# Three stick-breaking steps per pair of heads, and the first sparse unit at a higher priority

## Chip, cores and metric

The kernel runs on one core of a Trainium2 chip. The metric is the device time of one execution in microseconds. Five engines work side by side: TensorE (PE, matmuls; its weight loads are shown as PEld), VectorE (DVE), ScalarE (ACT), GpSimd (POOL) and SyncE (SP, which issues most transfers). Sums of matmuls lie in PSUM, which the kernel divides into eight banks of 128 x 512 values: two called `acc`, four called `S`, one `o` and one `tp`.

## What is computed

Two layers, each with two token mixers on the same normalised input of 512 tokens by 1024. The reference, cut to what matters:

```python
def stick_breaking_attention(q, k, v):           # 8 heads of 64
    for i in range(s_len // Q_BLOCK):
        ...
        z = einsum('bhqd,bhkd->bhqk', qb, kb) * scale
        mask = s[None, :] < t[:, None]
        log_1m = where(mask, log_sigmoid(-z), 0.0)
        between = cumsum(log_1m, axis=3, reverse=True) - log_1m
        w = where(mask, exp(log_sigmoid(z) + between), 0.0)
        outs.append(einsum('bhqk,bhkd->bhqd', w, vb))

def nsa_attention(...):                          # 8 query heads, 2 key heads
    kc, vc = compress_blocks(...)                # 31 blocks, two-layer MLP
    p_cmp = masked_softmax(q @ kc)               # o_cmp = p_cmp @ vc
    ...                                          # selected blocks: all 8 are taken
    o = gates[0] * o_cmp + gates[1] * o_slc + gates[2] * o_win

def hybrid_layer(x, ...):
    proj = rms_norm(x, norm_g) @ w_in            # 5912 columns
    y_a = merge_heads(o_a) * silu(sb_z)
    y_b = o_b * silu(n_z)
    merged = sigmoid(gate_a) * (y_a @ w_up_a) + sigmoid(gate_b) * (y_b @ w_up_b)
    return x + merged @ w_out
```

## The kernel before

Tokens stand along the columns and channels along the partitions. The projections are made from weights split into a high part `whi` (a cast on GpSimd or ScalarE, L162 and L404) and a low part `wlo` (VectorE, L404), three matmuls per block of 128 channels, into the banks `acc`. `w_ahead` keeps three splits ahead of TensorE.

A layer has three stages. In the first, the stick-breaking of four pairs of heads runs beside projections; in the second, the sparse attention of four query heads per key head runs beside the gate projections; in the third come the up projection and the output projection.

TensorE's order is written out by the kernel: `Pacer` counts estimated microseconds (`tick`), holds generators of projections (`fill`) and a list of steps that fall due after a given latency (`due`). `pump(us)` takes fill until that much planned time has gone by; `until` takes fill until a condition holds. The other engines' instructions are put in order by priority: `high_priority(offset=...)` moves them ahead of what has a smaller offset, PRIO is 300, PRIO_SB 600, PRIO_EV 900.

**Stick-breaking.** A pair of heads has four steps, from key block 3 (128 query columns) to block 0 (512). Step t makes the logits (`sb_qk`: two heads, a correction and a main matmul each, in one bank S per head), after which VectorE takes the mask's minimum (L903), ScalarE makes |z|, exp and log(1 + .) (L904 to L906), and VectorE adds (L907) into `e`. `sb_split` splits `e` into high and low parts and adds up, on GpSimd, the columns of the blocks seen (`sum`). `sb_cs` subtracts sums on TensorE with a triangular matrix for the own block and a matrix of ones for the blocks above, and ScalarE makes the weights `w`. `sb_pv` multiplies with the values into bank o. The loop at the end of the listing runs one round per step: values of step t-2, logits of step t, `X_GAP[0]` of fill, sums of step t-1, split of step t, `X_GAP[1]` of fill; 18 rounds with 3.5 + 3.4 planned us.

**Value tiles and compression.** `prep_vs` makes the stick's values `vS` (tile `gv`) in two halves, each of four token tiles (`proj_tok`), which VectorE evacuates at L659. `prep_cmp` lays out the compression's input (`f_t`, L691, 16 additions a layer), `prep_mlp`, `mlp_act`, `mlp_t`, `mlp_w2` and `mlp_k` are its chain down to the compressed keys `kC` (L799 to L803), with latencies `LAT` between them. `norm_rope` normalises a projection; its `rest` step uses the bank tp, and so do `mlp_t`, `mlp_w2`, `mlp_k` and `cmp_qk`.

**Passage to the sparse stage.** After the loop come `cmp_qk(0)`, the compression scores, and `nsa_qk(0, UNITS[0])`, the logits of the first unit (query blocks 0 and 1), which fill four banks S: two key heads by two query blocks. For each key head VectorE masks (L1047) and takes maxima (L1048), ScalarE makes exponentials `pr` (L1055), VectorE scales (L1065). `Y_LAT` planned us later the next unit's logits take the banks.

## Time and profile before

| | us |
|---|---|
| median of three runs (1001.96 to 1002.39) | 1002.15 |
| the profiled execution | 1003.2 |
| its span, first to last instruction | 1001.5 |
| TensorE busy | 967.7 |
| VectorE busy | 701.9 |
| ScalarE busy | 467.3 |
| GpSimd busy | 208.9 |

In the profile a line names source line, engine, operation, and the tiles as out<-in. "Idle before" is the time in which the engine stood still before an instruction, with what ended it. Ends of matmuls are modelled, so two matmuls in a row seem to overlap. The granted clock of TensorE is given as a share of 2.4 GHz.

### The profile page before, as it was taken

What the parts mean: (1) busy time and instruction counts of PE and PEld (TensorE: products, weight loads), DVE (VectorE), ACT (ScalarE), POOL (GpSimd) and SP (SyncE); (2) the same over time, 40 slices, a digit from 0 to 9 for tenths busy, and PEclk for the clock granted to TensorE, in tenths of its full rate; (3) what the DMA queues carried; (4) which work ended last, traced back from release to release, by engine and by line L of the source; (5) the groups of instructions that cost most, each with busy time, mean ns of one, the idle gap of its engine ahead of it and who ended that gap; (6) DMA issues with size and microseconds to landing.
All of it is one profiled execution on the core that took longest, in us unless ns stands there. A gap on an engine that the chain in (4) does not pass through costs nothing.

```text
span 1001.5 us, 14850 instructions
## 1 busy us (share of the span) xinstructions
PE 967.7 (97%) x5315; PEld 769.1 (77%) x5315; DVE 701.9 (70%) x1398; ACT 467.3 (47%) x1139; POOL 208.9 (21%) x256
## 2 busy tenths in 40 slices
PE   6999999989999999999999999999899999999998
PEld 4776767767888888888888787686688888888886
DVE  6778758779968875566565985587996887655631
ACT  5656355554543444533343535565453544344321
POOL 4153235431101111000012532343111101100000
PEclk9999999898999999999999999999899999999999
DMA  9433246422212222353643224363222221224331
GB/s 284 118 90 100 59 126 156 101 64 53 64 47 60 64 64 63 85 144 98 189 122 95 85 80 124 102 144 93 52 61 64 64 54 53 64 85 143 89 116 53
DMA packets 167530, 94.36 MB, mean 94 GB/s; under 512 B 39568, under 2 KB 160672, under 8 KB 167456
## 3 DMA queue, kind: packets, MB, share of 16 engines
q1 hardware_dynamic: 163120, 88.14, 32.7%
q10 hardware_dynamic: 3632, 3.17, 1.3%
q0 software_dynamic: 704, 2.11, 0.5%
q8 instruction: 42, 0.69, 0.3%
q14 instruction: 32, 0.26, 0.1%
HBM read 80.81 MB, written 6.29 MB: 87 GB/s over the span
## 4 chain that ended last, share of the span: by engine, by line
PE 76%; DVE 13%; ACT 6%; issue 3%; DMA 1%; POOL 1%; SPq 0%; ACTq 0%; DVEq 0%; POOLq 0%
PE acc L345 48%; PE S L345 16%; PE o L345 6%; PE tp L349 4%; DVE f_t L691 2%; DVE wlo L404 2%; PE tp L345 2%; ACT e L215 1%; ACT e L905 1%; DVE sX L505 1%; DVE hl L590 1%; DVE spl L923 1%; DVE sp L923 1%; DMA x_sb<-in_x_dram 1%; DVE e L907 1%
## 5 line engine op out<-in xcount | busy, mean ns | idle before, releaser
L345 PE MATMUL acc<-hh,whi 128*128 128x512 f32 x640 | 257.2, 402 | 0.1
L345 PE MATMUL acc<-hl,whi 128*128 128x512 f32 x640 | 255.0, 399 | 1.7 <-DVE hl L590 1.4
L345 PE MATMUL acc<-hh,wlo 128*128 128x512 f32 x640 | 181.7, 408 | 0.0
L162 POOL TENSOR_SCALAR whi<-raw 128x1024 fp32r<-128x1024 f32 (+1 forms) x84 | 95.0, 1130 | 400.1 <-PE acc L345 322.3
L404 DVE TENSOR_TENSOR wlo<-raw,whi 128x1024 fp32r<-128x1024 f32 (+1 forms) x124 | 154.9, 1249 | 32.7 <-POOL whi L162 23.0
L345 PEld LDWEIGHTS acc<-hl,whi 128*128 128x128 f32 x640 | 120.6, 188 | 27.4 <-DVE hl L590 3.4
L345 PEld LDWEIGHTS acc<-hh,whi 128*128 128x128 f32 x640 | 120.8, 189 | 26.3 <-issue 2.5
L345 PEld LDWEIGHTS acc<-hh,wlo 128*128 128x128 f32 x640 | 119.4, 191 | 27.6 <-issue 3.6
L404 ACT CAST whi<-raw 128x1024 fp32r<-128x1024 f32 x40 | 42.0, 1050 | 128.0 <-PE acc L345 47.5
L1078 ACT ACTIVATE pT<-tp 128x512 f32<-128x512 f32 x80 | 48.1, 601 | 102.5 <-PE tp L349 101.5
L1055 ACT ACTIVATE pr<-S,mx 128x256 f32<-128x256 f32 x192 | 81.9, 446 | 17.4 <-DVE mx L1048 10.3
L1048 DVE TENSOR_REDUCE mx<-S 128x2 f32<-128x512 f32 (+1 forms) x96 | 55.3, 593 | 11.8 <-PE S L345 11.7
L215 ACT ACTIVATE e<-S 128x128 f32<-128x128 f32 (+3 forms) x64 | 25.3, 435 | 80.4 <-DVE S L903 76.3
L345 PE MATMUL acc<-whi,hh 128*128 128x256 f32 (+1 forms) x192 | 58.0, 302 | 3.6 <-DVE gv L659 3.3
L1065 DVE TENSOR_SCALAR pr<-pr,rc 128x128 f32<-128x128 f32 (+3 forms) x128 | 55.0, 471 | 1.1
L345 PE MATMUL acc<-wlo,hh 128*128 128x256 f32 (+1 forms) x192 | 55.7, 290 | 0.0
L345 PE MATMUL acc<-whi,hl 128*128 128x256 f32 (+1 forms) x192 | 55.6, 290 | 0.0
L345 PE MATMUL S<-yh,wlo 128*128 128x512 f32 x128 | 50.7, 396 | 0.0
L345 PE MATMUL S<-yh,whi 128*128 128x512 f32 x128 | 50.7, 396 | 0.0
L345 PE MATMUL S<-yl,whi 128*128 128x512 f32 x128 | 50.1, 392 | 0.0
L349 PE MATMUL tp<-identf,pr 128*128 128x128 f32 x320 | 49.3, 277 | 0.0
L345 PE MATMUL S<-kN,nX 64*128 64x512 f32 (+1 forms) x192 | 42.2, 407 | 6.8 <-ACT pr L1055 6.8
(316 smaller groups left out, 1778.2 us busy)
## 6 DMA issues: line engine op xcount, KB each, us to landing
raw<-in_w_in_dram SPq DMA_DIRECT2D x72, 512.0 KB, 3.9
raw<-in_w_in_dram SPq DMA_DIRECT2D x36, 256.0 KB, 3.7
raw<-in_cmp_w_dram SPq DMA_DIRECT2D x16, 512.0 KB, 4.1
raw<-in_w_out_dram SPq DMA_DIRECT2D x16, 512.0 KB, 4.1
raw<-in_w_up_a_dram SPq DMA_DIRECT2D x16, 256.0 KB, 3.2
raw<-in_w_up_b_dram SPq DMA_DIRECT2D x32, 128.0 KB, 3.3
gv<-xs SPq DMA_DIRECT2D x16, 256.0 KB, 2.8
sq<-xq SPq DMA_DIRECT2D x48, 64.0 KB, 2.0
```

Source lines behind the costliest of these rows:

```text
L162: G.tensor_scalar(dst, src, 1.0, 0.0, op0=ALU.mult, op1=ALU.add)
L215: ins = A.activation(dst, src, func, **kw)
L345: T.matmul(out, lhsT, rhs, start=start, stop=stop, **kw)
L349: T.transpose(out, in_, ident)
L404: for ins in (eng.copy(hi, rv), V.tensor_sub(lo, rv, hi.bitcast(F32))):
L505: V.tensor_sub(X[b, g], q[a], X[a, g].bitcast(F32))
L691: V.tensor_tensor(f_v[hf][t * HD:(t + 1) * HD, :, a, g, 0:NCMP], src[:, :, t, hf:hf + NCMP], pe_v[:, hf * 8:(hf + 1) * 8, t:t + 1].to_broa ...
L923: V.tensor_sub(sp[1], e[:, :n], sp[0].bitcast(F32))
L1048: V.tensor_reduce(mx[:, n, g], sb[g][n].rearrange("p (k t c) -> p t k c", t=2, c=P), axis=AX.XY, op=ALU.max, negate=True)
L1055: exps.append(A.activation(pr[g][:, o:o + b - a, t], sv[:, t], AF.Exp, bias=mx[:, 0 if one else n, g, t:t + 1], accum_out=dn[:, n, g, t:t ...
L1065: V.tensor_scalar(pr[g][:, o:e, t], pr[g][:, o:e, t], rc[:, n, g, t:t + 1], None, op0=ALU.mult)
L1078: A.activation(pT.rearrange("p g t q -> p (g t q)"), pt, AF.Copy)
```

## The change

- The stick's steps per pair become three (`STEPS`): blocks 3 and 2 side by side in one bank (128 and 256 columns), then block 1, then block 0. `sb_qk`, `sb_split`, `sb_cs`, `sb_sum` and `sb_pv` follow. The loop has 14 rounds with 4.6 + 4.1 planned us.
- `cmp_qk(0)` and the first unit's `nsa_qk` stand under offset 600, and the next unit falls due one planned us later.
- The first two value tiles of the first half use banks S.
- The first half of the feature blocks is put off as well, by 0.0 and 1.5 us, and the second by 5.0 and 7.0.
- `ht` and `hv2` share a tile of the pool `wk`. The zeroing of `kC` moves ahead of its evacuation, which stands under offset 900. Three latencies grow.

```diff
@@ -38,12 +38,13 @@
 PRIO = 300
...
 N_WARM = (3, 2, 2, 3)
-LAT = {'norm': 5.0, 'mlp_t': 9.0, 'mlp_w2': 3.5, 'mlp_k': 16.0, 'sb0': 3.8, 'sb': 4.5, 'ang': 1.5, 'sin': 0.5}
+LAT = {'norm': 5.0, 'mlp_t': 11.5, 'mlp_w2': 4.2, 'mlp_k': 16.0, 'sb0': 3.8, 'sb': 5.7, 'ang': 1.5, 'sin': 0.5}
 PRIO_SB = 600
 PRIO_EV = 900
-X_GAP = (3.5, 3.4)
+X_GAP = (4.6, 4.1)
+STEPS = ((3, 2), (1,), (0,))
 Y_GAP = 1.5
-F_GAP = ((6.0, 8.0), (5.0, 7.0))
+F_GAP = ((0.0, 1.5), (5.0, 7.0))
 Y_LAT = (9.8, 9.2, 10.2)
@@ -445,12 +446,12 @@
         yield from gemm(po, wh, wl, hs.hh, hs.hl)
...
 
-    def proj_tok(l, pieces, evac):
+    def proj_tok(l, pieces, evac, bank_of=lambda i: acc_bank()):
         n = sum(m for _, m in pieces)
...
         for i in range(NT):
-            po = acc_bank()
+            po = bank_of(i)
             sl = slice(i * P, (i + 1) * P)
@@ -659,7 +660,7 @@
                         V.tensor_scalar(vS[i][:, c * 256:(c + 1) * 256], po[:, :256], r_col[:, i:i + 1], None,
...
 
-                yield from proj_tok(l, VS_P[c], evac_s)
+                yield from proj_tok(l, VS_P[c], evac_s, lambda i: s_bank() if c == 0 and i < 2 else acc_bank())
                 done.add(("vs", c))
@@ -694,8 +695,8 @@
                                     pe_v[:, hf * 8:(hf + 1) * 8, t:t + 1].to_broadcast([HD, 8, NCMP]),
...
 
-                        block(0)
-                        pc.later(F_GAP[a][g], lambda block=block: block(1))
+                        pc.later(F_GAP[0][g], lambda block=block: block(0))
+                        pc.later(F_GAP[1][g], lambda block=block: block(1))
 
@@ -749,9 +750,10 @@
                     pt = t_bank()
...
                         tr(pt[:, t * P:(t + 1) * P], u1[:, t * P:(t + 1) * P], identf)
-                    ht = g_tile("w", n=256).rearrange("p (t c) -> p t c", t=2)
+                    h4 = wkt("h4")
+                    ht = h4[:, :256].rearrange("p (t c) -> p t c", t=2)
                     V.tensor_copy(ht.rearrange("p t c -> p (t c)"), pt[:, :256])
-                    hv2 = g_tile("w", n=256).rearrange("p (t a c) -> p t a c", t=2, a=2)
+                    hv2 = h4[:, 256:].rearrange("p (t a c) -> p t a c", t=2, a=2)
                     for t in range(2):
@@ -796,11 +798,13 @@
                     pt = t_bank()
...
                     ptv = pt[:, 0:HD].rearrange("p (g c) -> p g c", g=2)
+                    for g in range(2):
+                        V.memset(kC[(1 - g) * HD:(2 - g) * HD, g, 1].bitcast(F32), 0.0)
+                with tc.high_priority(offset=PRIO_EV):
                     A.activation(kC[:, :, 0], ptv, AF.Copy)
                     for g in range(2):
-                        a, b = slice(g * HD, (g + 1) * HD), slice((1 - g) * HD, (2 - g) * HD)
+                        a = slice(g * HD, (g + 1) * HD)
                         V.tensor_sub(kC[a, g, 1], ptv[a, g], kC[a, g, 0].bitcast(F32))
-                        V.memset(kC[b, g, 1].bitcast(F32), 0.0)
                     done.add("cmp")
@@ -885,89 +889,107 @@
                     V.tensor_mul(g, po, r_bc)
...
 
+            def sb_step(t):
+                j, s = t // len(STEPS), t % len(STEPS)
+                cols_of, n = [], 0
+                for kb in STEPS[s]:
+                    cols_of.append((kb, slice(n, n + S - kb * P)))
+                    n += S - kb * P
+                return j, s, cols_of, n
+
             def sb_qk(t):
-                j, kb = t // NT, NT - 1 - t % NT
+                j, s, cols_of, n = sb_step(t)
                 R = sb_in[j]
-                n = S - kb * P
-                ks = slice(kb * P, (kb + 1) * P)
                 zb = [s_bank() for _ in range(2)]
-                for h, z in enumerate(zb):
-                    gs = slice(h * HD, (h + 1) * HD)
-                    mm(z[:, :n], R.sK2[gs, ks], R.sX[gs, h, kb * P:], True, False, n * .00022)
-                for h, z in enumerate(zb):
-                    mm(z[:, :n], R.sK1[:, h, ks], R.sX[:, h, kb * P:], False, True, n * .00043)
+                for kb, c in cols_of:
+                    ks = slice(kb * P, (kb + 1) * P)
+                    for h, z in enumerate(zb):
+                        gs = slice(h * HD, (h + 1) * HD)
+                        mm(z[:, c], R.sK2[gs, ks], R.sX[gs, h, kb * P:], c.start == 0, False, (S - kb * P) * .00022,
+                           skip_group_check=True)
+                for kb, c in cols_of:
+                    ks = slice(kb * P, (kb + 1) * P)
+                    for h, z in enumerate(zb):
+                        mm(z[:, c], R.sK1[:, h, ks], R.sX[:, h, kb * P:], False, True, (S - kb * P) * .00043,
+                           skip_group_check=True)
                 with tc.high_priority(offset=PRIO_SB):
...
                         e = g_tile("e")
-                        V.tensor_tensor(z[:, :P], z[:, :P], mk_sb, op=ALU.min)
+                        m = len(cols_of)
+                        zd = z[:, :m * P].rearrange("p (m c) -> p m c", m=m)
+                        V.tensor_tensor(zd, zd, mk_sb[:, None, :].to_broadcast([P, m, P]), op=ALU.min)
                         act_exp(e[:, :n], z[:, :n], AF.Abs)
...
                         R.e[h] = e
-                R.z[kb] = zb
+                R.z[s] = zb
 
             def sb_split(t):
-                j, kb = t // NT, NT - 1 - t % NT
+                j, s, cols_of, n = sb_step(t)
                 R = sb_in[j]
-                n = S - kb * P
                 with tc.high_priority(offset=PRIO_SB):
...
                         e = R.e[h]
-                        sp = [g_tile(f"sp{t}0", F32R) if kb == 0 else px.tile([P, n], F32R, tag=f"sp{t}{kb}", name="sp", bufs=2)
+                        sp = [g_tile(f"sp{t}0", F32R) if s == 2 else px.tile([P, n], F32R, tag=f"sp{t}{s + 1}", name="sp", bufs=2)
                               for t in "hl"]
-                        ins = A.activation(sp[0], e[:, :n], AF.Copy)
+                        ins = A.activation(sp[0][:, :n], e[:, :n], AF.Copy)
                         for i in w_last:
                             order(ins, i)
-                        V.tensor_sub(sp[1], e[:, :n], sp[0].bitcast(F32))
-                        R.sp[h, kb] = sp
-                        if kb == NT - 1:
+                        V.tensor_sub(sp[1][:, :n], e[:, :n], sp[0][:, :n].bitcast(F32))
+                        R.sp[h, s] = sp
+                        if s == 0:
                             R.sum[h] = px.tile([P, 2 * P], F32, tag="sum", name="sum", bufs=2)
-                            copy_pool(R.sum[h][:, P:], e[:, :P])
-                        elif kb > 0:
-                            G.tensor_add(R.sum[h][:, P * (kb - 1):], R.sum[h][:, P * (kb - 1):], e[:, P:n])
-                            if kb == 2:
-                                copy_pool(R.sum[h][:, :P], e[:, :P])
+                            G.tensor_add(R.sum[h][:, P:], e[:, :P], e[:, 2 * P:n])
+                            copy_pool(R.sum[h][:, :P], e[:, P:2 * P])
+                        elif s == 1:
+                            G.tensor_add(R.sum[h], R.sum[h], e[:, P:n])
 
             def sb_cs(t):
-                j, kb = t // NT, NT - 1 - t % NT
+                j, s, cols_of, n = sb_step(t)
                 R = sb_in[j]
-                n = S - kb * P
-                R.w[kb] = []
+                R.w[s] = []
                 for h in range(2):
-                    z = R.z[kb][h]
-                    for kk in (kb + 1, kb) if kb < NT - 1 else (kb,):
-                        off = (kk - kb) * P
+                    z = R.z[s][h]
+                    sp = R.sp[h, s]
+                    if s == 0:
+                        parts = [(ntri, sp, slice(0, P), slice(0, P)), (nones, sp, slice(0, P), slice(2 * P, 3 * P)),
+                                 (ntri, sp, slice(P, 3 * P), slice(P, 3 * P))]
+                    else:
+                        parts = [(nones, R.sp[h, s - 1], slice(P * (2 - s), 3 * P), slice(P, n)),
+                                 (ntri, sp, slice(0, n), slice(0, n))]
+                    for m, (tri, src, a, b) in enumerate(parts):
                         for u in range(2):
-                            mm(z[:, off:n], ntri if kk == kb else nones, R.sp[h, kk][u], False,
-                               kk == kb and u == 1, 0.04 + (n - off) * .00034, skip_group_check=True)
+                            mm(z[:, b], tri, src[u][:, a], False, m == len(parts) - 1 and u == 1,
+                               0.04 + (b.stop - b.start) * .00034, skip_group_check=True)
                     w = g_tile("w")
...
                         w_last.append(act_exp(w[:, :n], z[:, :n], AF.Exp))
-                    R.w[kb].append(w)
-                if 0 < kb < NT - 1:
+                    R.w[s].append(w)
+                if s < 2:
                     for h in range(2):
-                        sb_sum(R, h, kb, n - P)
-
-            def sb_sum(R, h, kb, n):
-                h0, l0 = (u[:, P:] for u in R.sp[h, kb])
-                s = R.sum[h][:, P * (kb - 1):] if kb == 2 else R.sum[h]
+                        sb_sum(R, h, s)
+
+            def sb_sum(R, h, s):
+                c = slice(2 * P, 3 * P) if s == 0 else slice(P, 3 * P)
+                h0, l0 = (u[:, c] for u in R.sp[h, s])
+                sm = R.sum[h][:, P:] if s == 0 else R.sum[h]
                 with tc.high_priority(offset=PRIO_SB):
-                    copy_pool(h0, s)
-                    G.tensor_sub(l0, s, h0.bitcast(F32))
+                    copy_pool(h0, sm)
+                    G.tensor_sub(l0, sm, h0.bitcast(F32))
 
             def sb_pv(t):
-                j, kb = t // NT, NT - 1 - t % NT
+                j, s, cols_of, n = sb_step(t)
                 R = sb_in[j]
-                n = S - kb * P
-                if kb == NT - 1:
+                if s == 0:
                     R.o = o_bank()
-                for h in range(2):
-                    gs = slice(h * HD, (h + 1) * HD)
-                    mm(R.o[gs, kb * P:], vS[kb][:, (2 * j + h) * HD:(2 * j + h + 1) * HD], R.w[kb][h][:, :n],
-                       kb == NT - 1, kb == 0, n * .0009, skip_group_check=True)
-                if kb == 0:
+                for kb, c in cols_of:
+                    for h in range(2):
+                        gs = slice(h * HD, (h + 1) * HD)
+                        mm(R.o[gs, kb * P:], vS[kb][:, (2 * j + h) * HD:(2 * j + h + 1) * HD], R.w[s][h][:, c],
+                           kb == NT - 1, kb == 0, (S - kb * P) * .0009, skip_group_check=True)
+                if s == 2:
                     if j:
@@ -1164,16 +1186,16 @@
                 pc.later(LAT["sb0"] if l else 6.0, lambda: done.add(("sb", 0)))
...
                 pc.fill.extend([fills[kind](a) for kind, a in X_FILL])
-                NS = 4 * NT
+                NS = 4 * len(STEPS)
                 for t in range(NS + 2):
                     if t >= 2:
-                        pc.until(lambda: ("vs", (t - 2) // (2 * NT)) in done)
+                        pc.until(lambda: ("vs", (t - 2) // (NS // 2)) in done)
                         sb_pv(t - 2)
                     if t < NS:
-                        j = t // NT
+                        j = t // len(STEPS)
                         pc.until(lambda: ("sb", j) in done)
                         R = sb_in[j]
-                        if t % NT == 0:
+                        if t % len(STEPS) == 0:
                             R.sp, R.z, R.w, R.e, R.sum = {}, {}, {}, {}, {}
@@ -1186,10 +1208,11 @@
             with ExitStack() as ly:
...
                 pc.fill.extend([fills[kind](a) for kind, a in Y_FILL])
-                sc = cmp_qk(0)
                 NU = len(UNITS)
-                pr = {0: nsa_qk(0, UNITS[0])}
-                ready = pc.now + Y_LAT[0]
+                with tc.high_priority(offset=PRIO_SB):
+                    sc = cmp_qk(0)
+                    pr = {0: nsa_qk(0, UNITS[0])}
+                ready = pc.now + Y_LAT[0] + 1.0
                 o, pTs = None, None
```

## Rows read from the trace of the kernel before

**Rows 1.** Page, busy time of each engine: us, share of the span, instructions.

```profile
PE 967.7 (97%) x5315; PEld 769.1 (77%) x5315; DVE 701.9 (70%) x1398; ACT 467.3 (47%) x1139; POOL 208.9 (21%) x256
```

**Rows 2.** Stretches: us, busy us (instructions) of each engine, TensorE's clock, DMA.

```profile
43.00:225.00 182.00, 174.19 (x915) 131.74 (x914) 135.31 (x237) 99.25 (x234) 74.72 (x89) 0.98 0.37 97
225.00:235.00 10.00, 7.69 (x34) 5.73 (x32) 10.00 (x30) 5.45 (x21) 2.10 (x2) 0.98 0.26 52
235.00:400.00 165.00, 164.83 (x1063) 134.03 (x1064) 127.58 (x313) 73.94 (x239) 20.30 (x19) 0.98 0.23 60
526.00:706.00 180.00, 176.91 (x974) 136.75 (x973) 132.32 (x238) 95.73 (x230) 68.17 (x90) 1.00 0.39 102
```

**Rows 3.** TensorE's waits over the span: us in total, times, longest us.

```profile
PE S L345 <- ACT pr L1055: 6.8, 4, 2.6
PE acc L345 <- DVE gv L659: 3.3, 4, 1.2
PE tp L345 <- DVE kC L802: 2.7, 1, 2.7
PE tp L349 <- DVE mlp_u L744: 2.6, 1, 2.6
PE o L345 <- ACT w L215: 1.5, 2, 1.2
PE tp L345 <- DVE w L753: 0.9, 1, 0.9
PE S L345 <- DMA sK<-sK: 0.8, 1, 0.8
```

**Rows 4.** Timeline of TensorE, both passages: start us, us, instruction, [idle before].

```profile
219.55 1.51 PE L345 MATMUL S<-kN,nX 64*128 64x512 f32 x8
...
234.12 0.38 PE L345 MATMUL S<-kN,nX 64*128 64x256 f32 x1 [1.81 <-ACT pr L1055]
...
235.17 2.15 PE L345 MATMUL S<-kN,nX 64*128 64x256 f32 x5 [0.66 <-ACT pr L1055]
...
714.85 0.38 PE L345 MATMUL S<-kN,nX 64*128 64x256 f32 x1 [2.58 <-ACT pr L1055]
...
716.95 2.16 PE L345 MATMUL S<-kN,nX 64*128 64x256 f32 x5 [1.72 <-ACT pr L1055]
```

**Rows 5.** Timeline of VectorE around the passage of layer 0.

```profile
211.41 0.19 DVE L802 TENSOR_TENSOR kC<-tp,kC 64x32 fp32r<-64x32 f32 x1
...
228.53 1.22 DVE L404 TENSOR_TENSOR wlo<-raw,whi 128x1024 fp32r<-128x1024 f32 x1
...
232.34 0.68 DVE L1048 TENSOR_REDUCE mx<-S 128x2 f32<-128x512 f32 x1
...
233.86 0.41 DVE L1048 TENSOR_REDUCE mx<-S 128x2 f32<-128x256 f32 x1
```

**Rows 6.** Timeline of ScalarE, last exponential of each key head, unit 0.

```profile
227.51 0.37 ACT L1055 ACTIVATE pr<-S,mx 128x128 f32<-128x128 f32 x1
...
234.66 0.36 ACT L1055 ACTIVATE pr<-S,mx 128x128 f32<-128x128 f32 x1
```

**Rows 7.** Stretches around three falls of the clock, columns as in rows 2.

```profile
176.00:184.00 8.00, 6.32 (x29) 6.32 (x30) 4.96 (x12) 4.25 (x11) 2.56 (x5) 0.57 0.37 83
231.50:242.00 10.50, 8.03 (x28) 6.09 (x27) 8.32 (x19) 4.08 (x12) 2.11 (x2) 0.67 0.31 67
711.50:724.00 12.50, 8.20 (x30) 6.17 (x29) 10.39 (x26) 4.68 (x12) 2.06 (x2) 0.73 0.20 44
```

**Rows 8.** Timeline, scaling of unit 0 on VectorE, weight cast on GpSimd.

```profile
230.21 0.61 DVE L1065 TENSOR_SCALAR pr<-pr,rc 128x256 f32<-128x256 f32 x2
...
231.14 1.28 DVE L1065 TENSOR_SCALAR pr<-pr,rc 128x128 f32<-128x128 f32 x2
...
231.30 1.05 POOL L162 TENSOR_SCALAR whi<-raw 128x1024 fp32r<-128x1024 f32 x1 [4.53 <-PE acc L345]
```

**Rows 9.** Timeline of weight loads, first one of a visit in layer 0.

```profile
58.87 0.20 PEld L345 LDWEIGHTS o<-w,gv 128*64 128x64 f32 x4 [0.35 <-issue]
```

## The prediction

> **What bounds the kernel now.** I read the busy times first [rows 1]: TensorE works 97% of the span, the next engine (VectorE) 70%. So the order of the 5315 matmuls on TensorE sets the time, and a change can win only where TensorE stands still or runs at a lower clock. The stretches of the span come next [rows 2]. In the sparse stage (235 to 400) TensorE is busy 164.8 of 165 us: nothing to win. In the stick-breaking stage of layer 0 (43 to 225) it is idle 7.8 us, in that of layer 1 (526 to 706) 3.1 us, and in the ten us behind the former 2.3 us, while VectorE is busy for all 10.00 of them. Third, the list of TensorE's waits [rows 3]: the largest is for the exponentials of the sparse branch (`pr`), 6.8 us in four waits; then come `gv` 3.3, `kC` 2.7, `mlp_u` 2.6, `w` of the stick 1.5, `w` of the compression 0.9 and `sK` 0.8. Fourth, where the four `pr` waits lie [rows 4]: all at the passage from one stage to the next, 1.81 and 0.66 us in layer 0, 2.58 and 1.72 us in layer 1. Unit 0 fills all four banks S (from 219.55), and unit 1's logits need them back about 12 us later.
>
> Why the banks are late is seen on VectorE and ScalarE [rows 5, 6]. The exponentials of the first key head end at 227.9, those of the second only at 235.0, because its maxima (L1048) come at 232.34 and 233.86. In between VectorE does what nobody waits for: a weight split of 1.22 us at 228.53, rope and norm of later query heads, and the scaling of the first head. The clock adds to it [rows 7]: 0.67 over 10.5 us in layer 0 and 0.73 over 12.5 us in layer 1, that is 6.9 and 6.8 us at 1.2 instead of 2.4 GHz, which begin in these waits. A third such fall (0.57 over 8 us) begins in the `mlp_u` wait. The `kC` wait, as long, is followed by none, so a fall is likely after a gap of over 2 us but not sure.
>
> **The change part by part.** The sum is against the profiled execution, 1003.2 us (span 1001.5 and 1.7 around it); the median of the runs shown, 1002.15, is 1.05 below it.
>
> *Precedence for compression scores and unit 0* (offset 600), and one planner us more before unit 1. It adds no instruction. VectorE can do the second head's maxima right behind the first head's; what stood between them filled most of 226.7 to 232.3, so they come some 5 us earlier and the banks are free near 230, against 231.8 now and about 1 us later by the new due time. The wait goes with some 3 us of margin. Gross gain: 6.8 us of waits; of the low clock 6.9 and 6.8 us, some 1 us each lies in the waits, and the rest works at half speed and loses up to half, 2 x 2.9 us. Together 12.6. VectorE's scaling of two 128-column pieces, with a weight cast of 1.05 us on GpSimd inside it, took 1.28 us, where two pieces of 256 columns took 0.61 [rows 8]; one such delay of 0.7 us I leave standing per layer: 12.6 - 2 x 0.7 = 11.2, bounds 0 and 12.6. What is moved back is on VectorE: the norm chains of query heads 1 to 3 (used a unit or more later), and the weight splits (offset 300). TensorE needs a split only when its projection starts, and three are held ahead, so I cost it at nothing; if that cover fails, one split late is 1.22 us [rows 5]. The rest steps of the norms hold the one bank tp until VectorE's addition (offset 300), which now also stands behind the unit; cost 0, up to 1.2 us per layer by the same row.
>
> Beside this row stands a rule that speaks against the edit. The Trainium skill (SBUF — State Buffer, section "SBUF: two separate sides") says that VectorE and GpSimd share one port pair as an exclusive lock, so that the later one blocks for the whole instruction of the other; the row agrees. By it precedence in VectorE's queue is none over GpSimd: were three such casts met in each layer and the margin used up, the gain would be 12.6 - 6 x 0.7 = 8.4 and the time 988.
>
> *Latencies of the compression chain* (`mlp_t` 9.0 to 11.5, `mlp_w2` 3.5 to 4.2), its tiles `ht` and `hv2` in `wk` and no longer in the stick's `w`. `mlp_u` came 2.6 us late, and 2.5 more planner us cover nearly that; the fall of the clock there leaves 5.9 us of work at half speed, up to 2.9 us. Gross 5.5, taken 4.0; bounds 0 (the chain only moves along) and 5.5. The `w` wait of 0.9: taken 0.7, bounds 0 and 0.9.
>
> *`kC`: memset ahead and the evacuation at offset 900.* The last of its subtractions ended at 211.6, behind splits of the stick [rows 5], and held the bank tp for 2.7 us. Taken 2.0, bounds 0 and 2.7: the chain now falls due 3.2 planner us later (31.7 for 28.5) while the stage's fill, and so its end, stays, so the next user of tp and the compression scores are closer behind it.
>
> *First two value tiles in banks S.* They no longer wait for the banks acc that the first query and key projections hold. Of `gv`'s 3.3 us in four waits the longest, 1.2 [rows 3], lies before the third of these tiles; the other 2.1 are in the second half of the values, which the edit leaves in acc. The first stick logits come earlier by that and then meet their key copy, so I take 0.8, bounds 0 and 1.2. The new spacing of the feature blocks (`F_GAP`) spreads 16 VectorE additions per layer that stood before those other evacuations: taken 1.0, bounds -1 and 2.1.
>
> *Three steps for four.* TensorE's matmuls stay the same in number and columns: 16 for logits, 28 for sums and 8 calls for values per pair, blocks 3 and 2 merely issued together. What goes is one visit in four: 4 per layer, 8 in all. A visit costs its switch; the nearest row is the 0.35 us that the weight load stood idle at one [rows 9]. 8 x 0.35 = 2.8 at most; weight loads between the two blocks stay, so I take 1.5, bounds 0 and 2.8. ScalarE and VectorE get five and three wide instructions per head and pair less; that is off the path, and I cost it at nothing. The waits for the stick's `w` (1.5) get a planner gap of 4.1 instead of 3.4 in front of the values: taken 1.0, bounds 0 and 1.5. `sK` with 5.7 instead of 4.5: taken 0.8, bounds 0 and 0.8.
>
> *New waits.* Every place of a fill is shifted, so buffers and VectorE meet differently. No row shows this. The nearest are the two layers with the same program but different waits, 7.8 and 3.1 us of idle time [rows 2]; the difference, 4.7, is about what a mere shift is worth. I add 5.0 for both layers, bounds 0 and 16 (both as bad as layer 0).
>
> The sum: 11.2 + 4.0 + 0.7 + 2.0 + 0.8 + 1.0 + 1.5 + 1.0 + 0.8 = 23.0 gained, 5.0 lost: 18.0 net. 1003.2 - 18.0 = 985.2, or 984.2 against the median; I say 985.
>
> **The rivals.** *The precedence is placed and does not help* (the second head's maxima still stand behind the first head's scaling, which has the same offset, or unit 1 finds its banks still taken). For it speaks that the scaling is part of the same unit [rows 8]; against it that it waits for ScalarE while the maxima are ready. Then 11.2 is not won: 985 + 11 = 996.
>
> *The waits come back elsewhere*: the stick's stages each show as much idle time as layer 0's, and the clock falls in one or two. New waits of 16 instead of 5: 985 + 11 = 996, and with a boundary only half repaired, 1001 to 1002: no change that shows.
>
> *Slower: the first step of three is late at every pair.* It now carries 384 columns where a step of 128 opened the pair, two blocks share a bank, and the sums' first matmuls cannot start before both are through masks, three activations and a split. For it speaks that TensorE already waited for the stick's `w`, at most 1.2 us [rows 3]; against it the gaps of 4.6 and 4.1 for 3.5 and 3.4. Price: 1.2 us at each of 12 visits in two layers is 29 us: 985 + 29 = 1014. It decides against the change from 0.75 us per visit (18 / 24).
>
> *Everything found goes and nothing comes*: 1003.2 - 23.0 = 980; with all gains at their upper bounds (30 us), 973.
>
> **How the numbers follow.** Forecast as summed (979 to 992): 0.60. All gains without new waits (973 to 979, or 980): 0.10. Precedence without effect (993 to 998): 0.14. Waits elsewhere (996 to 1004): 0.10, half of it without a difference that shows. Slower: 0.06. The predicted time is 985. From 977 to 999 holds the forecast, half of the case below it, the rival of the precedence and part of the next: 0.8 with the unknown costs' bounds. A difference of 0.2%, 2 us, is about what a measurement of this kernel can tell from none. Faster 0.88, same 0.05, slower 0.07.
>
> **What would show it.** Right, if the list of waits has no `pr`, `mlp_u` and `kC` wait over 1 us; if the clock is 1.00 at both passages; if the maxima of the second head stand within 3 us of the first's on VectorE; if TensorE still has 5315 matmuls (or a few missing records) with the same busy time per form. Wrong, if `pr` stays in the list, if a wait for `w`, `sp` or `e` of the stick recurs at each pair, if weight splits (`wlo`) become releasers of TensorE behind the passage, or if the idle time of the two stick stages exceeds 11 us in sum.

## The result and the profile after

The changed kernel takes 988.36 us (median of 4 runs, 987.51 to 989.61) where the kernel before takes 1002.23 (the three runs shown ahead and one more): a ratio of 0.9863, 95% interval 0.9846 to 0.9880, so some 14 us less. 985 was forecast. The profiled execution took 989.1 us with a span of 987.4. Most lines of the changed kernel have moved by one to some twenty numbers: L346 is TensorE's matmul, L472 the square of `norm_rope`, L497 its last addition, L1070 the maxima, L1077 the exponentials and L1087 the scaling of a sparse unit. Names that come up in the lists of waits: `zt` is the product by which VectorE empties a bank acc of the gate projections (L866), `rc` the factor of a unit's scaling (L1084), `sc` the compression scores (last operation L1019), and `pT` and `pcT` are transposed weights that ScalarE copies out of a bank.

The page's busy times answer to [rows 1]: the same 5315 matmuls, less of everything else.

```profile
PE 959.1 (97%) x5315; PEld 764.4 (77%) x5315; DVE 693.5 (70%) x1350; ACT 461.1 (47%) x1059; POOL 201.7 (20%) x240
```

TensorE's list of waits (us in total, times, longest) answers to [rows 3]:

```profile
PE tp L346 <- ACT sq L472: 9.0, 2, 4.5
PE acc L346 <- DVE gv L660: 3.0, 2, 2.4
PE tp L350 <- DVE pr L1087: 1.7, 2, 1.4
PE S L346 <- DMA sK<-sK: 0.6, 2, 0.4
```

The waits of `pr` at the banks S, of `mlp_u`, `kC` and the two `w` are gone. In their place stands above all one wait that was not there before: 4.5 us in each layer, for the square `sq`. The stretches (columns as in [rows 2]: the stage, the 20 us behind the passage with its first 11 apart, the sparse stage; then layer 1) show where it lies:

```profile
43.00:205.00 162.00, 161.46 (x886) 124.11 (x886) 121.86 (x201) 93.21 (x189) 65.59 (x80) 1.00 0.40 104
205.00:216.00 11.00, 6.49 (x26) 4.37 (x26) 10.85 (x37) 5.49 (x20) 0.00 (x0) 0.85 0.17 48
205.00:225.00 20.00, 15.49 (x57) 11.44 (x58) 17.56 (x47) 7.98 (x24) 3.96 (x3) 0.83 0.26 64
225.00:387.00 162.00, 161.64 (x1064) 130.84 (x1062) 127.15 (x305) 72.98 (x235) 21.16 (x20) 1.00 0.24 61
514.00:684.40 170.40, 167.76 (x940) 130.01 (x938) 121.12 (x200) 88.74 (x184) 65.65 (x80) 1.00 0.40 104
684.40:704.00 19.60, 15.10 (x60) 11.07 (x59) 17.07 (x44) 7.36 (x23) 3.42 (x3) 0.91 0.21 52
```

The stick's stages are nearly tight (0.5 us idle in layer 0, 2.6 in layer 1, at full clock); the 20 us behind each passage hold 4.5 us of standing still, and the clock falls there to 0.83 and 0.91. The late matmul on TensorE's timeline, in both layers:

```profile
214.34 2.08 PE L346 MATMUL tp<-sq,blk 128*128 128x512 f32 x2 [4.51 <-ACT sq L472]
693.81 1.89 PE L346 MATMUL tp<-sq,blk 128*128 128x512 f32 x2 [4.50 <-ACT sq L472]
```

What made it late in layer 0, on VectorE's timeline:

```profile
205.71 0.68 DVE L496 TENSOR_TENSOR sq<-sq,sin_t 128x512 f32<-128x512 f32 x1
...
212.47 0.42 DVE L1070 TENSOR_REDUCE mx<-S 128x2 f32<-128x256 f32 x1
212.88 0.68 DVE L497 TENSOR_TENSOR sq<-yy,sq 128x512 f32<-128x512 f32 x1
```

and on ScalarE's:

```profile
213.69 0.59 ACT L472 ACTIVATE sq<-acc 128x512 f32<-128x512 f32 x1
```

The rotary embedding of query head 1 has its sine product at 205.71, but its addition only at 212.88, behind the last maxima of unit 0. That addition frees a tile of the pool `wk`; the square of query head 3 has to have it (213.69), and TensorE, which is to sum that square, stands until 214.34. The precedence did what it says: unit 0's last maxima come at 212.5, its last exponential ends at 213.7, and unit 1's logits take the banks at 225.5 without a wait (ScalarE, then TensorE):

```profile
213.35 0.36 ACT L1077 ACTIVATE pr<-S,mx 128x128 f32<-128x128 f32 x1
...
225.48 1.51 PE L346 MATMUL S<-kN,nX 64*128 64x512 f32 x8
```

What it went past is now waited for.

Where the time came from, by landmarks of TensorE's timelines (us from the start of the span; first logits of the stick, first logits of unit 0, in both layers):

| kernel | stick, layer 0 | unit 0, layer 0 | stick, layer 1 | unit 0, layer 1 | span |
|---|---|---|---|---|---|
| before | 41.3 | 219.6 | 529.1 | 699.6 | 1001.5 |
| after | 39.9 | 204.9 | 516.2 | 684.4 | 987.4 |

Before, 178.3 us lie between the first two marks, after, 165.0. At the passage of layer 0 the changed kernel is 14.7 us ahead, at the end 14.1. Most of the gain, 13.3 us, is won in the stick's stage of layer 0. That of layer 1 wins 2.3, but what follows each passage takes longer than before: 1.8 us more from unit 0 of layer 0 to the stick of layer 1, and 1.1 more from unit 0 of layer 1 to the end.

### The profile page after: what moved, and what is told of

Its sections match the earlier page's. It is cut to its first block, busy times and chain, and to the rows that moved or that the text cites. A ratio compares the mean times of both kernels' runs of the same rounds, so it can differ in the third digit from the quotient of the medians.

```text
span 987.4 us, 14685 instructions
## 1 busy us (share of the span) xinstructions
PE 959.1 (97%) x5315; PEld 764.4 (77%) x5315; DVE 693.5 (70%) x1350; ACT 461.1 (47%) x1059; POOL 201.7 (20%) x240
## 4 chain that ended last, share of the span: by engine, by line
PE 86%; DVE 9%; DMA 2%; ACT 2%; issue 1%; SPq 0%; POOL 0%; DVEq 0%; POOLq 0%; ACTq 0%
PE acc L346 56%; PE S L346 18%; PE o L346 6%; PE tp L350 4%; PE tp L346 2%; DVE wlo L405 1%; DVE f_t L692 1%; DVE hl L591 1%; DVE pr L1087 1%; DMA sq<-xq 1%; DMA mpos_i<-in_positions_dram 1%; DMA sK<-sK 0%; DVE sq L497 0%; DVE mx L1070 0%; DVE sq L496 0%
## 5 line engine op out<-in xcount | busy, mean ns | idle before, releaser
L346 PE MATMUL acc<-hh,whi 128*128 128x512 f32 x640 | 257.4, 402 | 0.5 <-DVE gv L660 0.5
L346 PE MATMUL acc<-hl,whi 128*128 128x512 f32 x640 | 256.0, 401 | 1.2 <-DVE hl L591 1.2
L163 POOL TENSOR_SCALAR whi<-raw 128x1024 fp32r<-128x1024 f32 (+1 forms) x84 | 99.1, 1179 | 423.0 <-PE acc L346 330.1
L346 PE MATMUL acc<-hh,wlo 128*128 128x512 f32 x640 | 181.1, 407 | 0.0
L346 PEld LDWEIGHTS acc<-hh,wlo 128*128 128x128 f32 x640 | 120.1, 192 | 30.3 <-issue 6.2
L346 PEld LDWEIGHTS acc<-hl,whi 128*128 128x128 f32 x640 | 120.8, 189 | 27.6 <-issue 2.5
L346 PEld LDWEIGHTS acc<-hh,whi 128*128 128x128 f32 x640 | 120.8, 189 | 27.0 <-issue 2.3
L1077 ACT ACTIVATE pr<-S,mx 128x256 f32<-128x256 f32 x192 | 82.5, 448 | 28.1 <-DVE mx L1073 13.1
L1070 DVE TENSOR_REDUCE mx<-S 128x2 f32<-128x512 f32 (+1 forms) x96 | 55.6, 593 | 15.0 <-PE S L346 14.8
L1087 DVE TENSOR_SCALAR pr<-pr,rc 128x128 f32<-128x128 f32 (+3 forms) x128 | 54.0, 459 | 1.4
L346 PE MATMUL S<-yh,wlo 128*128 128x512 f32 x128 | 50.7, 396 | 0.0
L346 PE MATMUL S<-yh,whi 128*128 128x512 f32 x128 | 50.7, 396 | 0.0
L346 PE MATMUL S<-yl,whi 128*128 128x512 f32 x128 | 50.1, 392 | 0.0
L346 PE MATMUL acc<-whi,hh 128*128 128x256 f32 (+1 forms) x160 | 46.7, 292 | 2.4 <-DVE gv L660 2.4
L350 PEld LDWEIGHTS tp<-identf,pr 128*128 128x128 f32 x320 | 39.0, 140 | 12.8 <-DVE pr L1087 2.6
L216 ACT ACTIVATE e<-S 128x384 f32<-128x384 f32 (+1 forms) x48 | 23.0, 525 | 54.0 <-DVE S L921 53.7
L346 PE MATMUL acc<-wlo,hh 128*128 128x256 f32 (+1 forms) x160 | 45.7, 285 | 0.0
L346 PE MATMUL acc<-whi,hl 128*128 128x256 f32 (+1 forms) x160 | 45.7, 285 | 0.0
```

The lines of the kernel that those rows point to most:

```text
L163: G.tensor_scalar(dst, src, 1.0, 0.0, op0=ALU.mult, op1=ALU.add)
L216: ins = A.activation(dst, src, func, **kw)
L346: T.matmul(out, lhsT, rhs, start=start, stop=stop, **kw)
L350: T.transpose(out, in_, ident)
L1070: V.tensor_reduce(mx[:, n, g], sb[g][n].rearrange("p (k t c) -> p t k c", t=2, c=P), axis=AX.XY, op=ALU.max, negate=True)
L1077: exps.append(A.activation(pr[g][:, o:o + b - a, t], sv[:, t], AF.Exp, bias=mx[:, 0 if one else n, g, t:t + 1], accum_out=dn[:, n, g, t:t ...
```

## The experiments

Each ratio is against the kernel before, run on the same chip.

| run | edit | median, us | ratio (95%) |
|---|---|---|---|
| e1_rope | after; rotary operations at offset 900 | 985.34 | 0.9832 (0.9811 to 0.9852) |
| e2_q3tile | after; own tiles for query head 3 | 989.40 | 0.9866 (0.9838 to 0.9894) |
| e3_noprec | after without the precedence | 987.84 | 0.9855 (0.9834 to 0.9877) |
| e4_prec_alone | before with the precedence | 994.99 | 0.9925 (0.9904 to 0.9946) |
| e5_steps_alone | before with the three steps | 997.52 | 0.9952 (0.9938 to 0.9965) |
| e6_all_but_steps | after without the three steps | 988.67 | 0.9869 (0.9856 to 0.9883) |
| e7_chain_alone | before with the compression chain's edits | 994.15 | 0.9913 (0.9898 to 0.9928) |
| e8_rope_pool | after; rotary operations on GpSimd | 991.06 | 0.9885 (0.9872 to 0.9899) |
| e9_later_norm | after; head 3's sum of squares later | 982.39 | 0.9808 (0.9789 to 0.9828) |
| e10_later_norm_rope | e9 and e1 together | 982.63 | 0.9811 (0.9791 to 0.9830) |
| e11_tile_and_later | e9 and e2 together | 986.42 | 0.9845 (0.9824 to 0.9866) |
| e12_unit_first | e11, scores without precedence | 991.29 | 0.9895 (0.9878 to 0.9913) |

### What the new wait is worth: e1 to e4

The first theory was: the addition that stands behind unit 0 makes the wait, and without that the time falls by both waits and the low clock behind them.

```diff
+            with tc.high_priority(offset=PRIO_EV):
-            V.tensor_mul(rot, rot, sin_t)
-            V.tensor_add(rot, qc, rot)
+                V.tensor_mul(rot, rot, sin_t)
+                V.tensor_add(rot, qc, rot)
```

> The changed kernel; the two last operations of every rope (product with the sine, addition) get the offset 900, nothing else. Theory: in the changed kernel the addition for query head 1 (L497, 212.88) stands behind unit 0 on VectorE, and the square for query head 3 (L472, 213.69) waits for the tile of wk that the addition frees; TensorE waits 4.5 us a layer for that square and loses some 2 us more a layer at half clock. Then the addition comes near 206.5, the square near 207, both waits go, and the time is 975 to 979. Rival: the square simply stands behind the unit's exponentials in ScalarE's queue, and the addition beside it is chance: then 987 to 990, both waits stay.

```diff
-                norm_rope(po, cols[:, 16 + l:17 + l], fin)
+                own = (g_tile("e"), g_tile("e")) if j == 3 else None
+                norm_rope(po, cols[:, 16 + l:17 + l], fin, own)
```

> The changed kernel with its priorities untouched; the two tiles of query head 3's norm (xq, sq) come from the stick's tiles e, free by then, and not from wk. Theory (the square waits for a tile of wk): both 4.5 us waits go without any priority being changed, 975 to 980. Rival (the order of ScalarE's queue holds it): the waits stay, 987 to 990.

e1 gave 985.3, between theory and rival, and e2 989.4, the rival's time. In both the waits for `sq` are gone, so the cause of that wait (the tile that query head 3 shares with query head 1's addition) is shown. But little or none of the time was won: 3 us in e1, nothing in e2. From the list of waits of e1:

```profile
PE tp L350 <- DVE pr L1088: 4.7, 4, 1.6
PE acc L346 <- DVE zt L867: 3.2, 2, 1.6
```

and of e2:

```profile
PE S L346 <- ACT pr L1077: 6.7, 2, 3.5
PE tp L350 <- ACT pcT L1028: 1.8, 2, 1.4
```

The 4.7 for `pr` in e1 were 1.7 in the changed kernel, so 6.2 us of waits are new in e1. In e2 8.5 came, nearly all of it new, where 9.0 for `sq` and 1.7 for `pr` had gone. So I asked what the precedence is worth at all, by taking it out of the changed kernel (e3) and by putting it alone into the kernel before (e4):

```diff
-                with tc.high_priority(offset=PRIO_SB):
-                    sc = cmp_qk(0)
-                    pr = {0: nsa_qk(0, UNITS[0])}
-                ready = pc.now + Y_LAT[0] + 1.0
+                sc = cmp_qk(0)
+                pr = {0: nsa_qk(0, UNITS[0])}
+                ready = pc.now + Y_LAT[0]
```

> The changed kernel without the precedence (offset and the extra planned us taken back), all else as changed. Theory: the precedence removes the pr waits with their fall of the clock (12.6 us at most before) and brings 9.0 us of new waits with 3 to 4 us of half clock, so it is worth about nothing here: 985 to 992, pr waits of 5 to 8 us in the list, no wait for sq. Rival: it is worth the 11.2 us of the forecast and the waits for sq come from the shorter loop: 997 to 1001, with both kinds of wait in the list.

> The kernel before with the precedence alone (and its planned us). Theory: same trade, pr waits gone, waits for sq of 3 to 5 us a layer with half clock behind them: 998 to 1004. Rival (the trade needs the three steps): no wait for sq, 989 to 993.

The longest of TensorE's waits for another engine in e3:

```profile
PE S L346 <- ACT pr L1077: 8.8, 3, 4.3
```

and from the list of e4:

```profile
PE tp L345 <- DVE kC L802: 2.7, 1, 2.7
...
PE tp L349 <- DVE mlp_u L744: 2.6, 1, 2.6
...
PE tp L349 <- DVE pr L1065: 1.9, 2, 1.2
```

Within the change the precedence is worth nothing that can be measured (987.8 without it, 988.4 with it): 8.8 us of `pr` are exchanged for 9.0 us of `sq`. Alone it is worth 7.5 us (5.4 to 9.6 by the interval), 995.0 us between the two expectations, and e4 has no wait for `sq`. So the precedence by itself does not make that wait: another part of the change has to come with it.

### The parts alone: e5 to e7

e5 has the hunks of `STEPS`, `X_GAP` and the `sb_` functions alone; e6 all others; e7 only the compression chain's:

```diff
-LAT = {'norm': 5.0, 'mlp_t': 9.0, 'mlp_w2': 3.5, ...
+LAT = {'norm': 5.0, 'mlp_t': 11.5, 'mlp_w2': 4.2, ...
...
+                    h4 = wkt("h4")
+                    ht = h4[:, :256].rearrange("p (t c) -> p t c", t=2)
...
+                with tc.high_priority(offset=PRIO_EV):
                     A.activation(kC[:, :, 0], ptv, AF.Copy)
```

> The kernel before with the three steps and their planner gaps and nothing else. Theory (the sum's terms for the steps, 1.5 + 1.0, and the waits of before otherwise in place): 997 to 1001, with the pr waits at the passage still some 6 to 9 us. Rival (the steps carry what the precedence did not, because their work comes off VectorE and ScalarE and shortens the stick stages' wait chains): 990 to 995, and the mlp_u or kC wait gone with nothing done to their latencies.

> Everything of the change except the three steps and their gaps. Theory (steps worth about 2.5, the rest of the measured 14 lies in the other edits): 989 to 993. Rival (the steps carry half of the gain): 994 to 999. The square's wait of 4.5 us (tp <- sq) should be there if the precedence makes it alone, and absent if it takes the steps' earlier stage end to make it.

> The kernel before with the compression chain's edits alone: the three latencies' mlp part, the shared tile h4, the zeroing ahead and the evacuation of kC at offset 900. Theory (terms 4.0 + 0.7 + 2.0): 993 to 998, without an mlp_u or kC wait over 0.5 us and without the fall of the clock at 176 to 184. Rival (the chain only moves along and the waits come back at its next links): 999 to 1003.

From TensorE's waits of e5:

```profile
PE S L346 <- ACT pr L1074: 8.8, 3, 4.3
PE tp L350 <- DVE mlp_u L745: 4.3, 1, 4.3
...
PE S L346 <- DMA sK<-sK: 1.4, 1, 1.4
```

of e6, where `sq` L471 is not in the list:

```profile
PE tp L349 <- DVE pr L1068: 2.3, 3, 0.9
PE o L345 <- ACT w L215: 2.2, 4, 1.2
PE acc L345 <- DVE gv L659: 2.2, 3, 1.1
```

and of e7:

```profile
PE S L345 <- ACT pr L1058: 5.1, 3, 2.5
...
PE tp L345 <- DVE kC L806: 0.4, 1, 0.4
PE tp L349 <- DVE mlp_u L744: 0.3, 1, 0.3
```

The chain alone gives 8.7 us (7 to 10), as its theory said: `kC` 0.4 and `mlp_u` 0.3 are left of 5.3, and 176 to 184, which had a clock of 0.57 before [rows 7], has 1.00. The steps alone give 4.8 us (3.5 to 6.2), at the upper end of what their theory allowed, and that although they lengthen the waits for `pr` (8.8 for 6.8) and `mlp_u` (4.3 for 2.6) and have `sK` at 1.4. On the other side the waits for `kC` (2.7) and for the stick's `w` (1.5) are gone from e5's list, the former as the rival had it, with nothing done to its latency. Over the whole list the waits of e5 are no less than before, so the gain must lie in TensorE's own work. I added up, from the starts in its timelines, the time of all visits to the stick (from the first of its matmuls to the next matmul of something else, what the first one starts later than the spacing of the matmul ahead, less recorded idle time). Both have 240 such matmuls in each layer:

| | visits, layer 0 and 1 | time, us |
|---|---|---|
| e7 (four steps) | 34 + 36 | 46.4 + 43.7 = 90.1 |
| after (three steps) | 27 + 28 | 42.2 + 42.2 = 84.4 |

5.7 us for 15 visits less, 0.38 each. The two pairs of kernels that differ by the steps alone give much the same, 5.4 us between before and e5 and 5.5 between e6 and after (which spacing is taken off moves each of these sums by some tenths). That all of it lies in going to and fro, and none in the two blocks merged within a visit, is not shown. e6, everything but the steps, is as fast as the whole (988.67 and 988.36, a shade better than its theory's 989 to 993): what the steps win, something takes back. e6 shows what. Its unit 0 begins at 213.1. The same two operations as above on its VectorE:

```profile
209.44 0.69 DVE L495 TENSOR_TENSOR sq<-sq,sin_t 128x512 f32<-128x512 f32 x1
...
211.17 0.69 DVE L496 TENSOR_TENSOR sq<-yy,sq 128x512 f32<-128x512 f32 x1
```

and the square on its ScalarE:

```profile
212.67 0.59 ACT L471 ACTIVATE sq<-acc 128x512 f32<-128x512 f32 x1
```

There the addition (211.17) is done before unit 0 begins (213.1), and the precedence has nothing in its way. With three steps unit 0 begins at 204.9, 8 us earlier, and finds that addition undone. The wait takes both, the steps and the precedence: it is absent without the precedence (e3, e5) and without the steps (e4, e6). Whether the two suffice without the other edits no run shows.

### Order or backlog: e8 to e12

Two theories are left. *Order*: TensorE meets one late result, and has other work it could do first. *Backlog*: VectorE has more to do at the passage than there is time, so another of its results is late instead. e8 takes 4.1 us per layer off VectorE; e9 only moves TensorE's step (5 planner us later); the others go on from there.

```diff
# e8, query heads 1 to 3
-            V.tensor_mul(rot, rot, sin_t)
-            V.tensor_add(rot, qc, rot)
+            with tc.high_priority(offset=PRIO_EV if late else 0):
+                (G if late else V).tensor_mul(rot, rot, sin_t)
+                (G if late else V).tensor_add(rot, qc, rot)
# e9, query head 3
-        pc.later(LAT["norm"], rest)
+        pc.later(LAT["norm"] + late, rest)
# e12
-                with tc.high_priority(offset=PRIO_SB):
-                    sc = cmp_qk(0)
-                    pr = {0: nsa_qk(0, UNITS[0])}
+                sc = cmp_qk(0)
+                with tc.high_priority(offset=PRIO_SB):
+                    pr = {0: nsa_qk(0, UNITS[0])}
```

> The changed kernel with the sine product and the addition of the rotary embedding of query heads 1 to 3 on GpSimd, at offset 900, where GpSimd shows 0.00 us busy at both passages. It takes 4.1 us per layer (6 x 0.69) off VectorE. Theory (the passage is bound by VectorE's backlog, and whichever of its operations goes last makes TensorE wait): the tp <- sq wait of 4.5 falls below 1.5 in each layer and no other wait over 1.5 takes its place, 978 to 983. Rival (the waits only change their name, since the rest of the backlog or GpSimd's slower operations come late instead): 985 to 990.

> The changed kernel; only the step of query head 3 in which TensorE sums its squares falls due 10 instead of 5 planner us after the projection. No other engine's instruction order is meant to change, TensorE takes 5 us of projections first. Theory (the wait is one of order: TensorE meets the square 4.5 us too early and has other work): both 4.5 us waits for sq go and the two falls of the clock behind them, 975 to 980. Rival (VectorE's backlog at the passage is the bound, so TensorE meets the next of its late results instead): another wait of 3 us or more per layer within 25 us of the first, 985 to 990.

> As e9_later_norm, and the sine product and addition of the rotary embedding at offset 900 as in e1_rope, which alone gave 985.3. Theory (order alone): the square is early and TensorE late, so no wait for sq, and those that e1_rope showed for zt (1.6 per layer) come back at most in part: 974 to 980. Rival (backlog): as e1_rope, 983 to 987, with the waits for zt and pr of e1_rope in place.

> As e9_later_norm, and query head 3's two tiles come from the pool of e as in e2_q3tile, so that its bank acc is evacuated right behind its projection. Theory (in e9_later_norm the next projections waited 1.6 us per layer for zt because the third projection's bank was still held by the late square): the zt wait goes below 0.5, 978 to 981. Rival (the backlog of VectorE is what binds, and q3's chain now goes ahead of other work as in e2_q3tile): waits for pr of 2 us or more per layer within 40 us of the passage, 983 to 988.

> As e11_tile_and_later, and only the first unit stands under offset 600, no longer the compression scores, whose softmax of eight VectorE operations (2.7 us by their rows) nobody needs before some 20 us later. Theory (what is waited for is a matter of order): unit 0's maxima and scalings come 2 to 3 us earlier, no wait over 1 us at the passage, 977 to 981. Rival (backlog): the scores are late instead, a wait for sc or pcT of 2 us or more, and 982 to 988.

New in TensorE's waits of e8:

```profile
PE acc L346 <- DVE rc L1084: 4.5, 2, 2.2
...
PE tp L350 <- DVE pr L1088: 3.3, 2, 2.3
PE tp L346 <- ACT pT L1101: 3.0, 1, 3.0
```

of e9:

```profile
PE acc L346 <- DVE zt L866: 3.2, 2, 1.6
PE tp L350 <- DVE pr L1087: 3.1, 3, 1.4
```

of e11:

```profile
PE tp L350 <- DVE pr L1087: 7.2, 8, 2.6
```

and of e12:

```profile
PE tp L350 <- DVE sc L1019: 13.0, 2, 6.5
```

The 20 us behind the passage of layer 0, columns as in [rows 2], in e6:

```profile
213.10:233.10 20.00, 19.96 (x97) 15.58 (x97) 19.73 (x48) 10.45 (x29) 4.11 (x4) 1.00 0.20 43
```

in e9:

```profile
204.30:224.30 20.00, 18.43 (x89) 14.13 (x88) 19.84 (x50) 10.12 (x27) 3.40 (x3) 1.00 0.28 65
```

in e11:

```profile
204.80:224.80 20.00, 20.00 (x98) 15.79 (x98) 19.91 (x50) 11.18 (x29) 3.15 (x3) 1.00 0.26 59
```

and in e12:

```profile
204.60:224.60 20.00, 13.54 (x60) 10.31 (x59) 19.60 (x48) 7.87 (x24) 4.53 (x4) 0.92 0.29 67
```

VectorE is busy for 19.6 to 19.9 of 20 us in all four, whatever TensorE does. (In the changed kernel it is 17.56: 10.85 of the first 11 us, and less behind the late square.) A full VectorE fits the backlog but does not prove it, since in e6 TensorE stands for only 0.04 of its 20 us beside a VectorE as full. Three runs speak for the backlog. e8 (991.1, past the rival's 985 to 990) has two new names behind the passages, `rc` and `pT`, and 3.3 for `pr` where 1.7 stood; but it also loads GpSimd, which costs VectorE time (last section). In e11 (986.4, the rival's) TensorE works 20.00 of the first 20 us, without a wait for `zt`, and then, from 234, waits 2.6 us for the scaling of a later unit. In e12 (991.3, worse than both) the scores, taken out of the precedence, come 6.5 us late in each layer. Yet e9, which takes no operation off VectorE, wins 6 us over the changed kernel (982.4 for 988.4) and ends between the two expectations: 9.0 us of waits for `sq` went, 3.2 for `zt` and 1.4 more for `pr` came. So order is worth about half of the waits, and the other half comes back. e10 (982.6) adds nothing to e9 and also ends between its two expectations (974 to 980 and 983 to 987); its list has `pr` with 3.2 and `zt` with 2.2.

None of these orders is without a wait within some 35 us behind the passage while it begins at 204 to 205; whether one exists stays open. That VectorE's full 20 us cause what comes back is argued from these lists; no run took enough work off VectorE, without loading GpSimd, to show it. e9 beats both kernels: 19 us (17 to 21) less than before.

## Why the prediction held, point by point

The time lay 3.4 us from the forecast. That is in part luck: the largest term was 11 us too high, and several others, wrong the other way, made up for most of it.

- **The precedence (11.2).** Right: the four `pr` waits at the banks are gone, with a margin of 12 us and not 3 (last exponential done at 213.7, banks taken at 225.5). Much of that margin is the new wait itself, which holds TensorE up: in e9, without it, the banks are taken at 219.5, 5 us behind the last exponential (214.4). Wrong is the step that cost what is moved back at nothing ("the norm chains of query heads 1 to 3 (used a unit or more later)"). I looked at who uses their result, not at the tile that their last addition frees and the square that waits for it. The bank tp, which I named with up to 1.2 us per layer, was not it. Counted with the wait that it makes, the term measured about 0 within the change (e3); alone 7.5, inside its bounds of 0 and 12.6.
- **Three steps (1.5).** Mis-sized. The price of a visit was right (0.35 from [rows 9], 0.38 measured), the count was not: a step goes to the stick twice, once for values and logits and once for sums, so 15 visits went and not 8. It measured 5.7 (5.4 and 5.5 in the pairs that differ by the steps alone), twice the upper bound of 2.8.
- **The stick's `w` (1.0).** 1.5: the wait is gone.
- **Compression chain and `kC` (4.0 + 0.7 + 2.0 = 6.7).** Right in kind, 2 us too small: 8.7 alone, interval 7.2 to 10.2, the low clock of [rows 7] included. In e7 the waits for `pr` are also 1.7 us shorter (5.1 for 6.8), so not all of it need be the chain's own.
- **Value tiles and `F_GAP` (0.8 + 1.0).** 0.3 by the list of waits. The first stick logits come 1.4 us earlier, and of the three waits before 115 us one of 0.55 is left. But in the second half of layer 1's values a wait that was 1.1 is now 2.4. e5, without these edits, has it with 2.1, and e6, with them but without the steps, still has 1.1, so it comes with the steps; in e6 `gv` is 1.1 less than before.
- **`sK` (0.8).** 0.2: 0.6 us are left in two waits.
- **New waits (5.0, bounds 0 and 16).** 1.7 for `pr` beside the 9.0 for `sq`, which stand in the first point already. Counted here they make 10.7, and more with the low clock behind them: a term of the right kind, at the upper part of its bounds, and at the passage rather than spread.

The measured terms, 0 + 5.7 + 1.5 + 8.7 + 0.3 + 0.2 - 1.7 = 14.7, stand against 14.1 between the two profiled executions (1003.2 and 989.1). The forecast's 18.0 was 4 too high: the precedence brought 11 less than summed and the value tiles 1.5 less; the visits brought 4 more, the chain 2 more, and the new waits beside `sq` cost 3 less. That these terms add up to within 0.6 us should not be leaned on. They come from different runs, and putting the loss down to the precedence is a choice: beside all the rest the steps are worth as little (988.7 without them in e6, 987.8 without the precedence in e3, 988.4 with both).

Of the rivals, the slower one is refuted: no wait for `w`, `sp` or `e` recurs at a pair. "The precedence has no effect" was true of the time, not of its mechanism, since unit 1 finds its banks free; 996 did not come because of the visits and the chain. "The waits come back elsewhere" is what happened, at the passages alone. Of the signs, the old waits went as named, but the clock is not 1.00 at the passages.

The rule of the Trainium skill (SBUF — State Buffer, section "SBUF: two separate sides") was put at 8.4 us for the precedence and 988 in all. The time is 988, but not for that reason: while the addition was overtaken, from 205 to 216, GpSimd was busy for 0.00 us.

## What to carry to other kernels

Precedence on an engine that is full for 20 us does not shorten its queue; before giving it, list which tiles and banks the overtaken operations free, and who waits for those. Two edits that each win alone can be worth no more together: one that ends a stage earlier moves its boundary into work that the other then overtakes. When TensorE meets a late result, try first to give TensorE something else, as in e9, and look for the next late result behind it.

## What the hardware showed

GpSimd's work lengthens VectorE's where GpSimd begins first. In e8 VectorE's weight split took 2.26 us where GpSimd did an addition beside it, and 1.20 where it did nothing. GpSimd's timeline in e8:

```profile
203.94 1.27 POOL L498 TENSOR_TENSOR sq<-yy,sq 128x512 f32<-128x512 f32 x1
```

and VectorE's:

```profile
204.03 2.26 DVE L405 TENSOR_TENSOR wlo<-raw,whi 128x1024 fp32r<-128x1024 f32 x1 [2.43 <-PE acc L346]
...
215.38 1.20 DVE L405 TENSOR_TENSOR wlo<-raw,whi 128x1024 fp32r<-128x1024 f32 x1
```

Layer 1 shows the same, 2.32 us at 686.27. It goes the other way where VectorE begins first. In e8 a split takes its usual 1.22 us, and the weight cast on GpSimd that begins 0.07 later takes 2.04 where others take 1.05:

```profile
178.94 1.22 DVE L405 TENSOR_TENSOR wlo<-raw,whi 128x1024 fp32r<-128x1024 f32 x1
...
179.01 2.04 POOL L163 TENSOR_SCALAR whi<-raw 128x1024 fp32r<-128x1024 f32 x1 [2.37 <-PE acc L346]
```

The rule of the Trainium skill (SBUF — State Buffer, section "SBUF: two separate sides"), by which the one that begins first holds the shared ports and the other waits for its end, agrees with both: at 204 the later one lost 1.06 us, and the other still ran for 1.18. Work moved to an idle GpSimd is not free for VectorE: its next operation, the scores' first, started at 206.21 here and at 205.38 in the changed kernel.

The clock does not follow the length of a wait alone. In e9 TensorE's 1.57 us of wait at 213 is followed by full clock, 1.45 us at 236 by a fall (the two matmuls with the wait before them, then stretches, where the clock is the third number from the end):

```profile
212.96 0.47 PE L346 MATMUL acc<-hh,whi 128*128 128x512 f32 x1 [1.57 <-DVE zt L866]
...
236.35 0.72 PE L350 MATMUL tp<-identf,pr 128*128 128x128 f32 x2 [1.45 <-DVE pr L1087]
...
211.00:221.00 10.00, 8.43 (x39) 6.00 (x38) 9.84 (x26) 3.99 (x11) 1.05 (x1) 1.00 0.27 56
235.00:243.00 8.00, 6.58 (x26) 5.28 (x27) 6.44 (x15) 2.33 (x6) 1.34 (x1) 0.79 0.18 52
```

The second wait comes among transposes of 128 columns, the first among projections of 512. Why the clock fell after one and not after the other these runs do not settle. The prediction's "a fall is likely after a gap of over 2 us" is not borne out: here 1.45 us were followed by one, and before, the 2.7 us for `kC` by none.
